# The border into the output projection of a hybrid decoder layer: other buffers, earlier loads, retention started later

## The chip, the cores and the metric

The kernel runs on one core of a Trainium2 chip. The metric is the device time of one execution in microseconds; the lower the better. Of the core's engines four matter here: TensorE (PE in the profile; its weight loads are PEld) multiplies matrices into the eight banks of PSUM, VectorE (DVE) does elementwise work, ScalarE (ACT) does copies, casts and functions, and the SyncE queue (SP) issues every DMA of this kernel. Each of these works through its own queue in order. GpSimd has no part in the stretch that is changed.

## The reference, cut to what matters

One decoder layer on 1024 tokens of width 1024, float32. A pre-norm feeds one input projection with six column groups of 1024:

```python
xn = rms_norm(h, norm_in_g)
proj = xn @ w_in                                  # 1024 x 6144
q, k, v, g_ret, x_lru, g_lru = split(proj)
o_ret = group_norm_heads(chunkwise_retention(rotary(q), rotary(k) * HD ** -0.5, v))   # 8 heads x 128
y_ret = o_ret * silu(g_ret)
o_lru = rg_lru(causal_depthwise_conv(x_lru, conv_w, conv_b), ...)    # gates, decay, scan
y_lru = o_lru * silu(g_lru)
h = h + concat([y_ret, y_lru]) @ w_out            # 2048 x 1024
return rms_norm(h, norm_out_g)
```

The retention goes over 8 chunks of 128 tokens; per chunk and head it needs the masked scores q·k, their product with v, the product of q with a state, and an update of that state from k and v.

## The kernel before, in words

**Stages.** First v is projected (`v_phase`), with the weights of w_in streamed. Then 20 "quads" follow, each 256 columns of the other five groups for all tokens, done as seven half-size products (P1 to P7, a Strassen-like scheme) of 12 matmuls each; twelve quads are for the LRU group and the two gates, the last eight for q and k. One `Runner.step` of a quad does p2, p6, p5, p7, then p1 of the *next* quad, then p4 and p3, and between these prepares the next quad's weights (`prep1` to `prep4`: sums, and splits into a high and a low part). Results go to DRAM scratch: v to `v_d`, rotated q and k to `qk_d`, the gate to `g_d`, the LRU output to `l_d`.

**The output projection** (lines 699 to 947) multiplies 8 token tiles by w_out in four passes: LRU rows with output columns 0 to 511, LRU rows with columns 512 to 1023 (`dh` 0 and 1), retention rows with the first half of the columns, and retention rows with the second. One unit (`unit_o`) is one token tile in one pass: 8 values of k by 3 matmuls (high by high, high by low, low by high), so 24 matmuls of 128x512. A weight slab (`slab`) is 256 rows of w_out, loaded into a `wraw` buffer and split into a high tile by ACT (line 106) and a low tile by DVE (line 107) in the pool `wo`; four slabs make a pass. A token tile (`y_tile`) is loaded into a `wraw` buffer too, from `l_d` or from `o_d`, and split in the same way into the pool `yl`. There are three `wraw` buffers. The residual input (`h`, line 885) is loaded behind the latest token tile and added when a unit is done.

**Retention** runs inside the passes. `pieces` makes 35 closures out of the two head halves a and b (`Retention(0)`, `Retention(1)`): the first, `first(a, 0)`, does loads, scores (line 787), transposes of k (794) and the copy `kn` (797); the second does `state` (808) and `out` (825, 826) of a's chunk 0; later ones alternate, and `first(r, n)` also flips chunk n-1 (847), multiplies it by the gate and stores it to `o_d`. `unit_o` calls `fill` after k = 3 and after k = 7; each call takes one closure off the list.

**SBUF.** The buffers of the quads and of the output projection share the right side of SBUF. For the quads, in order of address and in KB a partition: the operands of P1, P2, P6, P5, P7, P4, P3 (16 each, four tiles of 4), `slabs` (36), `raw` (two of 8, the incoming w_in), `sums` (8). This stack is closed, and over it lie, in the same order of address: `qkc` (16, incoming q and k of retention), `wraw` (12), `wo` (40), `yl` (64), `vc` (8), `h` (32); the total is 172 both times. A buffer can be written as soon as the old tile under it has been read for the last time. The last quad reads P1 first (a step early), then P2, P6, P5, P7, P4, P3. The small buffers of retention (`kn`, `sm`, `gch`, ...) lie on the left side over `w4`, which holds the last quads' q and k until they are rotated and stored.

**Order.** The framework plans the order of each engine's queue by its own estimate of times: among the instructions whose operands and buffers are free by that estimate, it takes the one written first. One that is written late but ready early is issued early. `tc.issue_after` ties an instruction behind another.

```python
    ...
        ("qkc", 4), ("wraw", 3), ("wo", 10), ("yl", 16), ("vc", 4), ("h", 8))}
    ...
    w_o = group(D, 0)
    ...
    load_yl(0)
    while fillers:
        fill()
    ...
    fillers.extend(pieces(Retention(0), Retention(1)))
```

Of the kernel before, what the change touches and what calls it, by code (L numbers as in the profile page):

```python
# [10 lines left out]
F32 = mybir.dt.float32  # L11
F32R = mybir.dt.float32r
I32 = mybir.dt.int32
AF = mybir.ActivationFunctionType
ALU = mybir.AluOpType

P = 128
T = 1024
D = 1024
NT = T // P  # L20
NK = D // P
# [19 lines left out]
def hybrid_layer(  # L41
# [17 lines left out]
    pe, act, dve, pool, sp = nc.tensor, nc.scalar, nc.vector, nc.gpsimd, nc.sync  # L59
# [7 lines left out]
    def pool_on(side, name, bufs):  # L67
        return tc.tile_pool(name=name, bufs=bufs, side=side, reuse_waits="tile")

    const = ctx.enter_context(tc.tile_pool(name="const", bufs=1, side="left"))  # L70
    small = ctx.enter_context(tc.tile_pool(name="small", bufs=4, side="left"))
# [3 lines left out]
    def psum():  # L75
        return ps_p.tile([P, 512], F32, name="pp", tag="pp")
# [28 lines left out]
    def split(src, hi, lo):  # L105
        act.copy(out=hi, in_=src)  # L106
        dve.tensor_tensor(out=lo, in0=src, in1=hi.bitcast(F32), op=ALU.subtract)  # L107
# [41 lines left out]
    rstd = const.tile([P, NT], F32, name="rstd")  # L149
# [8 lines left out]
    o_d = dram.tile([NT, P, 2, 4, P], F32, name="o_d")  # L158
    l_d = dram.tile([8, P, T], F32, name="l_d")
# [4 lines left out]
    raw = s_stack.enter_context(pool_on("right", "raw", 2))  # L164
# [317 lines left out]
    fillers = []  # L482

    def fill():
        if fillers:
            f = fillers.pop(0)
            if f:
                f()
# [205 lines left out]
    run = Runner(lq + qk_quads())  # L694
    while run.i < len(run.q):
        run.step()
    s_stack.close()

    op = {n: ctx.enter_context(pool_on("right", n, k)) for n, k in (
        ("qkc", 4), ("wraw", 3), ("wo", 10), ("yl", 16), ("vc", 4), ("h", 8))}  # L700
    def slab(row, col):
        r = op["wraw"].tile([P, 2, 512], F32, name="wor", tag="wor")
        sp.dma_start(out=r, in_=w_out[row:row + 256, col:col + 512]
                     .rearrange("(k p) c -> p k c", p=P))
        hi, lo = [op["wo"].tile([P, 2, 512], F32R, name="wo", tag="wo") for _ in range(2)]
        split(r, hi, lo)
        return [(hi[:, j], lo[:, j]) for j in range(2)]

    def group(row0, col, ks=range(0, NK, 2)):
        return [a for k in ks for a in slab(row0 + k * P, col)]  # L710

    last_load = [None]

    def y_tile(src):

        r = op["wraw"].tile([P, NK, P], F32, name="yraw", tag="wor")
        last_load[0] = sp.dma_start(out=r, in_=src)
        hi, lo = [op["yl"].tile([P, NK, P], F32R, name="yt", tag="yt") for _ in range(2)]
        split(r, hi, lo)
        return hi, lo  # L720

    hres = []
    for t in range(NT):
        r = op["h"].tile([P, T], F32, name="h", tag="h")
        hres.append(r)

    def unit_o(ps, y, wg, cols, fills=True):
        for k in range(NK):
            mm3(ps, tuple(a[:, k] for a in y), tuple(a[:, cols] for a in wg[k]), k == 0, k == NK - 1)
            if fills and k in (3, 7):  # L730
                fill()

    w_o = group(D, 0)
    yl = {}

    def load_yl(t):
        yl[t] = y_tile(l_d[:, :, t * P:(t + 1) * P].rearrange("k p c -> p k c"))

    def load_yr(t):
        yl[t] = y_tile(o_d[t].rearrange("p f h c -> p (f h) c"))  # L740

    load_yl(0)
    while fillers:
        fill()
    ph_stack.close()
# [106 lines left out]
    def pieces(a, b):  # L852

        def first(r, n):
            if n < NT:
                r.scores(n)
            if n:
                r.flip(n - 1)

        f = []  # L860
        for n in range(NT + 1):
            m = n - 1
            f.append(lambda n=n: first(a, n))
            if m >= 0:
                f.append(lambda m=m: first(b, m))
            if n < NT:
                f.append(lambda n=n: (a.state(n), a.out(n)))
            if m >= 0:
                f.append(lambda m=m: (b.state(m), b.out(m)))
        return f + [None, lambda: first(b, NT)]  # L870

    fillers.extend(pieces(Retention(0), Retention(1)))
    for dh in range(2):
        cols = slice(dh * HALF, (dh + 1) * HALF)
        w_cur = w_o
        nxt = (D, HALF) if dh == 0 else (0, 0)
        w_o = group(*nxt, (0,))
        for t in range(NT):
            if dh == 0 and t + 1 < NT:
                load_yl(t + 1)  # L880
            ps = psum()
            unit_o(ps, yl[t], w_cur, slice(0, HALF))
            r = hres[t][:, cols]
            with tc.issue_after(last_load[0].ins):
                sp.dma_start(out=r, in_=x[t * P:(t + 1) * P, cols])
            dve.tensor_tensor(out=r, in0=ps, in1=r, op=ALU.add)
            if dh == 1 and 0 < t < NT - 2:
                load_yr(t - 1)
            if t == NT - 2:
                w_o += group(*nxt, (2, 4, 6))  # L890
# [5 lines left out]
    def square(dst, src):  # L896
        junk = junkp.tile([P, 512], F32, name="junk", tag="junk")
        act.activation(out=junk[:, :src.shape[-1]], in_=src, func=AF.Square, accum_out=dst)  # L898

    w_cur, w_o = w_o, group(0, HALF, (0,))  # L900
    for t in range(NT):
        if t < 2:
            load_yr(t + 5)
        elif t == 3:
            while fillers:
                fill()
            load_yr(NT - 1)
        elif t == NT - 2:
            w_o += group(0, HALF, (2, 4, 6))
        ps = psum()  # L910
        unit_o(ps, yl[t], w_cur, slice(0, HALF))
        r = hres[t][:, :HALF]
        m = ssum[:, t, 0:1]
        dve.tensor_tensor(out=r, in0=ps, in1=r, op=ALU.add)  # L914
        square(m, r)
        dve.tensor_scalar(out=m, in0=m, scalar1=1.0 / D, scalar2=EPS, op0=ALU.mult, op1=ALU.add)
        dve.tensor_tensor(out=r, in0=r, in1=gain2[:, :HALF], op=ALU.mult)
    for t in range(NT):
        r = hres[t][:, HALF:]
# [14 lines left out]
        root = small.tile([P, 1], F32, name="root", tag="root")  # L934
# [82 lines left out]
```

## Time and profile before

| what | value |
|---|---|
| time, median of 3 runs | 767.24 us (765.67 to 769.76) |
| the profiled execution's own time | 765.5 us |
| its span (first to last instruction) | 763.7 us |
| PE matmul busy | 734.1 us, 96% of the span |
| DVE busy | 548.6 us, 72% |
| ACT busy | 413.4 us, 54% |
| mean granted TensorE clock | 0.993 |

The share of a chain or an engine is a mean over stages. To read a stage one takes a window of it: busy time of each engine, granted clock, and how much of the 16 DMA engines was in use. The page's strip of 40 slices (19 us each) shows PE at nine tenths or more except at both ends, in the two slices from 496 to 535 us (6 and 8) and in the one from 649 to 668 us (8).

### The profile page before, as it was taken

The numbers are of one execution on the slowest core, as the hardware profiler recorded it, in microseconds if no ns is written. First come the engines' busy times: TensorE is split into PE (matmuls) and PEld (weight loads), VectorE is DVE, ScalarE is ACT, GpSimd is POOL, SyncE is SP. The second block draws the span as 40 slices with busy tenths as digits, with TensorE's granted clock in tenths as the row PEclk, the third lists the DMA queues.
The fourth block names the chain that finished last, engine by engine and source line by source line (L and its number), as shares of the span: only waits on it lengthen the run. The fifth ranks groups of instructions, "written<-read, shape, count | busy, mean of one in ns | idle before, by whom it ended". The sixth has DMA issues, their size and how long they took to land.

```text
span 763.7 us, 9411 instructions
## 1 busy us (share of the span) xinstructions
PE 734.1 (96%) x3508; PEld 610.8 (80%) x3508; DVE 548.6 (72%) x918; ACT 413.4 (54%) x635; POOL 0.2 (0%) x4
## 2 busy tenths in 40 slices
PE   6999999999999999999999999968999999899996
PEld 5877888887787788788788888757888898788885
DVE  6998647669977968977899888585567665652443
ACT  7784436695599679679533333255435443431332
POOL 0000000000000000000000000000000000000000
PEclk9999999999999999999999999999999999999999
DMA  9752712141214212421445542789946556331022
GB/s 317 268 191 88 245 53 70 56 128 38 72 52 161 74 55 87 148 83 52 169 122 126 134 110 56 226 266 323 313 146 206 194 179 235 97 129 36 28 88 106
DMA packets 85406, 105.58 MB, mean 138 GB/s; under 512 B 4848, under 2 KB 58224, under 8 KB 85360
## 3 DMA queue, kind: packets, MB, share of 16 engines
q1 hardware_dynamic: 85360, 104.99, 43.0%
q8 instruction: 27, 0.44, 0.2%
q14 instruction: 19, 0.16, 0.1%
HBM read 75.61 MB, written 29.36 MB: 137 GB/s over the span
## 4 chain that ended last, share of the span: by engine, by line
PE 67%; DVE 13%; ACT 10%; DMA 5%; issue 4%; SPq 0%; DVEq 0%; ACTq 0%
PE pp L112 59%; PE pp L826 2%; DVE xc L561 2%; PE pp L825 2%; PE pp L808 2%; PE pp L787 2%; DMA yraw<-l_d 2%; DVE wq L107 1%; ACT wq L106 1%; PE pp L847 1%; DVE y L614 1%; DVE wl L107 1%; DMA rot<-in_rot_t 1%; ACT L643 1%; PE pp L794 1%
## 5 line engine op out<-in xcount | busy, mean ns | idle before, releaser
L112 PE MATMUL pp<-wh,wq 128*128 128x512 f32 x960 | 301.6, 391 | 1.6 <-ACT cy L470 0.7
L112 PEld LDWEIGHTS pp<-wh,wq 128*128 128x128 f32 x960 | 179.9, 188 | 42.9 <-ACT cy L461 2.2
L112 PE MATMUL pp<-wo,yt 128*128 128x512 f32 (+1 forms) x792 | 186.1, 390 | 3.9 <-ACT yt L106 3.9
L112 PE MATMUL pp<-wl,wq 128*128 128x512 f32 x480 | 186.9, 389 | 0.0
L112 PEld LDWEIGHTS pp<-wo,yt 128*128 128x128 f32 x792 | 143.4, 189 | 31.6 <-ACT yt L106 4.3
L112 PEld LDWEIGHTS pp<-wl,wq 128*128 128x128 f32 x480 | 90.1, 188 | 18.5
L107 DVE TENSOR_TENSOR wq<-t,wq 128x1024 fp32r<-128x1024 f32 x40 | 48.7, 1221 | 39.1 <-ACT wq L106 32.1
L106 ACT CAST wq<-t 128x1024 fp32r<-128x1024 f32 x40 | 41.7, 1049 | 31.3 <-PE pp L112 26.7
L112 PE MATMUL pp<-wh 128*128 128x512 f32 x112 | 45.6, 407 | 8.0 <-ACT wh L106 8.0
L112 PE MATMUL pp<-wh,w 128*128 128x512 f32 x160 | 52.9, 391 | 0.1
L112 PE MATMUL pp<-wl,wh 128*128 128x512 f32 x112 | 44.8, 401 | 0.0
L112 PE MATMUL pp<-wh,wl 128*128 128x512 f32 x112 | 44.1, 398 | 0.0
L898 ACT ACTIVATE junk<-h 128x512 f32<-128x512 f32 (+1 forms) x17 | 10.3, 607 | 49.8 <-DVE h L914 25.3
L461 ACT COPY cy<-pp 128x512 f32<-128x512 f32 x20 | 11.6, 581 | 46.1 <-PE pp L112 45.5
L112 PEld LDWEIGHTS pp<-wh,w 128*128 128x128 f32 x160 | 30.0, 188 | 6.9 <-DVE w L107 0.6
L112 PEld LDWEIGHTS pp<-wh 128*128 128x128 f32 x112 | 21.8, 195 | 13.2 <-ACT wh L106 8.4
L112 PE MATMUL pp<-wl,w 128*128 128x512 f32 x80 | 31.1, 389 | 0.0
L839 ACT ACTIVATE yn<-pp,nb,rs_y 128x128 f32<-128x128 f32 x64 | 24.1, 458 | 11.8 <-DVE nb L837 11.8
L470 ACT COPY cy<-pp 128x512 f32<-128x512 f32 x20 | 11.6, 578 | 29.4 <-PE pp L112 29.3
L422 ACT CAST wq<-wraw 128x512 fp32r<-128x512 f32 x40 | 22.9, 617 | 8.3 <-PE pp L112 7.4
L97 ACT ACTIVATE rs_s<-ve 128x4 f32<-128x4 f32 x16 | 3.2, 202 | 43.8 <-DVE ve L832 43.8
L424 DVE TENSOR_TENSOR wq<-wraw,wq 128x512 fp32r<-128x512 f32 x40 | 26.7, 681 | 0.1
(154 smaller groups left out, 1116.2 us busy)
## 6 DMA issues: line engine op xcount, KB each, us to landing
wraw<-in_w_in SPq DMA_DIRECT2D x40, 512.0 KB, 4.7
qkc<-qk_d SPq DMA_DIRECT2D x16, 512.0 KB, 5.1
wor<-in_w_out SPq DMA_DIRECT2D x16, 512.0 KB, 5.7
bt<-in_w_in SPq DMA_DIRECT2D x20, 256.0 KB, 5.4
xA<-in_xT SPq DMA_DIRECT2D x16, 256.0 KB, 5.4
v_d<-vo SPq DMA_DIRECT2D x16, 256.0 KB, 2.4
xt<-in_x SPq DMA_DIRECT2D x8, 512.0 KB, 3.3
l_d<-y SPq DMA_DIRECT2D x8, 512.0 KB, 3.2
```

Source lines behind the costliest of these rows:

```text
L106: act.copy(out=hi, in_=src)
L107: dve.tensor_tensor(out=lo, in0=src, in1=hi.bitcast(F32), op=ALU.subtract)
L112: pe.matmul(ps, a, b, start=first and j == 0, stop=last and j == 2, skip_group_check=True)
L422: act.copy(out=h[:, j], in_=b)
L424: dve.tensor_tensor(out=l[:, j], in0=b, in1=h[:, j].bitcast(F32), op=ALU.subtract)
L461: act.copy(out=self.cy[:, :TH], in_=self.A)
L561: dve.scalar_tensor_tensor(out=xc[:, d:], in0=c[:, :T - d], scalar=cw[3 - d], in1=xc[:, d:], op0=ALU.mult, op1=ALU.add)
L787: heads(lambda h, hs: pe.matmul(psc[:, hs], k[:, hs], q[:, hs], start=True, stop=True))
L808: heads(lambda h, hs: pe.matmul(pkv[:, hs], kn[:, hs], vn[:, hs], start=True, stop=True))
L825: pe.matmul(po[:, hs], q[:, hs], st[:, h], start=True, stop=False)
L826: pe.matmul(po[:, hs], sm[:, h], vn[:, hs], start=st is None, stop=True)
L839: heads(lambda h, hs: act.activation(out=yn[:, hs], in_=po[:, hs], func=AF.Identity, scale=rs[:, h:h + 1], bias=nb[:, h:h + 1]))
```

## The change

The order of the pools on the right side becomes `wraw`, a new pool `y0` of two tiles, `wo`, `qkc`, `yl` (now 14), `vc`, `h`. So the staging buffers and the first token tile lie over the operands that the last quad reads first, and `qkc` moves from P1's place to the end of P5's and to P7's. Half of the first weights is loaded into a `raw` tile before the quads' stack is closed. The first token tile is loaded ahead of the weights, the second ahead of the loop. A square root of one column is written there as well. The first slab for the second pass is loaded in unit 2, not ahead of unit 0. Retention's list gets three empty entries, so its first closure comes in unit 1 and its second in unit 2, and the third and fourth closures change places. In the third pass the loads of token tiles 5 to 7 stand at units 0, 2, 4 (before: 0, 1, 3), and the rest of the list is emptied at unit 4.

```diff
+    early = raw.tile([P, 2, 2, 512], F32, name="early", tag="raw")
+    for j in range(2):
+        row = D + (4 + 2 * j) * P
+        sp.dma_start(out=early[:, j], in_=w_out[row:row + 256, 0:512].rearrange("(k p) c -> p k c", p=P))
     s_stack.close()
 
     op = {n: ctx.enter_context(pool_on("right", n, k)) for n, k in (
-        ("qkc", 4), ("wraw", 3), ("wo", 10), ("yl", 16), ("vc", 4), ("h", 8))}
-    def slab(row, col):
-        r = op["wraw"].tile([P, 2, 512], F32, name="wor", tag="wor")
-        sp.dma_start(out=r, in_=w_out[row:row + 256, col:col + 512]
-                     .rearrange("(k p) c -> p k c", p=P))
+        ("wraw", 3), ("y0", 2), ("wo", 10), ("qkc", 4), ("yl", 14), ("vc", 4), ("h", 8))}
+    def slab(row, col, r=None):
+        if r is None:
+            r = op["wraw"].tile([P, 2, 512], F32, name="wor", tag="wor")
+            sp.dma_start(out=r, in_=w_out[row:row + 256, col:col + 512]
+                         .rearrange("(k p) c -> p k c", p=P))
...
-    def y_tile(src):
-
+    def y_tile(src, t):
+
+        pl = "yl" if t else "y0"
...
-        hi, lo = [op["yl"].tile([P, NK, P], F32R, name="yt", tag="yt") for _ in range(2)]
+        hi, lo = [op[pl].tile([P, NK, P], F32R, name="yt", tag=pl) for _ in range(2)]
...
-    w_o = group(D, 0)
...
     load_yl(0)
+    w_o = group(D, 0, (0, 2))
+    for j in range(2):
+        w_o += slab(None, None, early[:, j])
+    load_yl(1)
+    act.activation(out=small.tile([P, 1], F32, name="root", tag="root"), in_=rstd[:, 0:1],
+                   func=AF.Sqrt)
     while fillers:
         fill()
...
-    fillers.extend(pieces(Retention(0), Retention(1)))
+    p_a, p_b, *rest = pieces(Retention(0), Retention(1))
+    rest[0], rest[1] = rest[1], rest[0]
+    fillers.extend([None, None, p_a, None, p_b] + rest)
     for dh in range(2):
...
-        w_o = group(*nxt, (0,))
+        if dh == 1:
+            w_o = group(*nxt, (0,))
         for t in range(NT):
-            if dh == 0 and t + 1 < NT:
+            if dh == 0 and 0 < t < NT - 1:
                 load_yl(t + 1)
+            if dh == 0 and t == 2:
+                w_o = group(*nxt, (0,))
...
-        if t < 2:
-            load_yr(t + 5)
-        elif t == 3:
+        if t == 4:
             while fillers:
                 fill()
-            load_yr(NT - 1)
+        if t in (0, 2, 4):
+            load_yr(t // 2 + 5)
         elif t == NT - 2:
```

## Rows read from the trace of the kernel before

**Rows 1.** Busy time of each engine in stretches around the border (the view by windows): stretch, its length, busy time and instructions of PE, PEld, DVE, ACT, POOL, then the granted clock, the share of the DMA engines in use and GB/s.

```profile
456.00:470.00 14.00, 14.00 (x64) 11.58 (x63) 11.88 (x15) 5.54 (x9) 0.00 (x0) 1.00 0.19 48
470.00:485.00 15.00, 15.00 (x68) 12.43 (x67) 8.47 (x10) 3.68 (x6) 0.00 (x0) 1.00 0.64 176
...
500.00:515.00 15.00, 9.02 (x38) 7.16 (x36) 13.09 (x13) 7.96 (x11) 0.00 (x0) 0.89 0.96 294
515.00:530.00 15.00, 11.68 (x71) 9.84 (x72) 7.50 (x21) 8.31 (x19) 0.00 (x0) 1.00 1.04 311
```

**Rows 2.** The same view, cut at the end of the last quad's last matmul, at the point from which PE is full again, and near the end.

```profile
500.30:533.30 33.00, 23.71 (x126) 19.88 (x127) 22.98 (x35) 18.09 (x32) 0.00 (x0) 0.95 1.01 310
...
533.30:657.30 124.00, 124.00 (x801) 111.72 (x800) 75.32 (x279) 52.42 (x132) 0.00 (x0) 1.00 0.62 204
...
671.80:757.00 85.20, 85.15 (x401) 71.26 (x399) 35.63 (x89) 25.15 (x56) 0.00 (x0) 1.00 0.22 78
```

**Rows 3.** Who waited for whom from 485 to 534 us: total us, times, longest.

```profile
ACT yt L106 <- DMA yraw<-l_d: 6.3, 4, 4.6
...
PE pp L112 <- ACT yt L106: 3.9, 1, 3.9
...
PE pp L847 <- ACT yn L839: 2.9, 1, 2.9
...
PE pp L808 <- ACT kn L797: 2.2, 1, 2.2
...
PE pp L112 <- ACT cy L470: 0.7, 1, 0.7
```

**Rows 4.** The group of the projection's matmuls among PE's groups from 500.3 to 533.3 us.

```profile
L112 PE MATMUL pp<-wo,yt 128*128 128x512 f32 x60 | 16.7, 422 | 3.9 <-ACT yt L106 3.9
```

**Rows 5.** Two pieces of the chain of waits where PE runs without a gap: start, length, what.

```profile
528.31 0.89 PE pp L787 x8
...
529.64 2.77 PE pp L112 x12
```

**Rows 6.** The SP queue in order of time: start, us, line, what it loads or stores.

```profile
476.23 1.99 SPq L772 DMA_DIRECT2D qkc<-qk_d  x3
485.52 1.41 SPq L703 DMA_DIRECT2D wor<-in_w_out  x3
...
496.73 0.37 SPq L703 DMA_DIRECT2D wor<-in_w_out  x1
497.87 0.37 SPq L717 DMA_DIRECT2D yraw<-l_d  x1
...
512.56 1.48 SPq L682 DMA_DIRECT2D qk_d<-cy  x1
...
518.29 0.84 SPq L772 DMA_DIRECT2D qkc<-qk_d  x2
```

**Rows 7.** DMA issues of the whole run: number, KB each, median us from issue to landing.

```profile
qkc<-qk_d SPq DMA_DIRECT2D x16, 512.0 KB, 5.1
wor<-in_w_out SPq DMA_DIRECT2D x16, 512.0 KB, 5.7
...
yraw<-l_d SPq DMA_DIRECT2D x8, 512.0 KB, 6.3
```

**Rows 8.** DVE in order of time: the reads of the `raw` tiles of the last two quads (lines 415 and 424), and the end of the last quad.

```profile
453.76 0.68 DVE L424 TENSOR_TENSOR wq<-wraw,wq 128x512 fp32r<-128x512 f32 x1
...
458.48 0.68 DVE L415 TENSOR_TENSOR t<-wraw 128x512 f32<-128x512 f32 x1
...
472.80 0.68 DVE L424 TENSOR_TENSOR wq<-wraw,wq 128x512 fp32r<-128x512 f32 x1
...
500.33 0.69 DVE L480 TENSOR_TENSOR cy<-pp,cy 128x512 f32<-128x512 f32 x1 [1.35 <-PE pp L112]
...
509.87 1.22 DVE L679 TENSOR_TENSOR cx<-cx,t 128x1024 f32<-128x1024 f32 x1
```

**Rows 9.** ACT in order of time; in brackets the idle time ahead and what ended it.

```profile
493.91 0.59 ACT L470 COPY cy<-pp 128x512 f32<-128x512 f32 x1 [4.85 <-PE pp L112]
...
521.95 1.28 ACT L97 ACT_TABLE_LOAD   x1
524.01 0.20 ACT L97 ACTIVATE rs_s<-ve 128x4 f32<-128x4 f32 x1 [0.78 <-DVE ve L832]
```

**Rows 10.** All engines in order of time where the second pass goes over into the third (an SP issue, an ACT cast, a PE transpose).

```profile
661.05 0.38 SPq L703 DMA_DIRECT2D wor<-in_w_out  x1
...
665.14 1.04 ACT L106 CAST wo<-wor 128x1024 fp32r<-128x1024 f32 x1 [2.17 <-DMA wor<-in_w_out]
...
666.60 0.33 PE L847 MATMUL pp<-ident,yn 128*128 128x128 f32 x1 [2.22 <-ACT yn L839]
```

**Rows 11.** Instructions in order of time from the start: a function of line 231, which is written behind the whole v stage; the two `diag` tiles of line 215, which are `raw` tiles; and the first load of a quad's weights into a `raw` tile.

```profile
2.49 0.21 ACT L231 ACTIVATE sp_a<-par_sb 128x8 f32<-128x8 f32 x1 [0.48 <-DMA par_sb<-in_par]
...
72.84 1.30 DVE L215 TENSOR_TENSOR diag<-ident,rstd 128x512 f32<-128x512 f32 x2
...
74.81 0.94 SPq L394 DMA_DIRECT2D wraw<-in_w_in  x2
```

**Rows 12.** The last retention tile: its store on SP, and the cast of the token tile that is loaded from it.

```profile
679.48 0.32 SPq L850 DMA_DIRECT2D o_d<-ot  x1
...
684.82 1.05 ACT L106 CAST yt<-yraw 128x1024 fp32r<-128x1024 f32 x1 [2.85 <-DMA yraw<-o_d]
```

More of the change, by code (lines that the diff above doesn't have):

```diff
@@ L731, in unit_o @@
                 fill()
-    w_o = group(D, 0)
     yl = {}
     def load_yl(t):
-        yl[t] = y_tile(l_d[:, :, t * P:(t + 1) * P].rearrange("k p c -> p k c"))
+        yl[t] = y_tile(l_d[:, :, t * P:(t + 1) * P].rearrange("k p c -> p k c"), t)
     def load_yr(t):
-        yl[t] = y_tile(o_d[t].rearrange("p f h c -> p (f h) c"))
+        yl[t] = y_tile(o_d[t].rearrange("p f h c -> p (f h) c"), t)
     load_yl(0)
+    w_o = group(D, 0, (0, 2))
[4 more added lines that the diff above has]
+                   func=AF.Sqrt)
     while fillers:
```

## The prediction

> **What bounds the kernel now.** I read the busy time by stretch first. PE is busy without a gap before 493 us, again from 533 to 657 us, and from 672 us to the last unit [rows 1, 2]. There the time is the number of matmuls, and nothing that another engine does matters until it makes PE wait. So the change can only give what PE loses in between, and can only cost where it makes new holes. The big hole is 500.3 to 533.3 us: 33.0 us with 23.7 us busy, 9.3 us idle [rows 2]. The waits say at whom: 3.9 us at the first matmul of the projection, for the cast of the first token tile; 2.2 us for retention's `kn`; 2.9 us for `yn`; and a little ahead of it 0.7 us for a copy of the last quad [rows 3]. ACT is behind all of them, and ACT itself waited 6.3 us for token tiles to land. The SP queue says why they land late: staging lies over P2's operands, so the first three slabs are issued at 485.5 us, the next one at 496.7 and the first token tile at 497.9 [rows 6], while the DMA engines were in use at 0.19 and 0.64 before and at 0.96 to 1.04 afterwards [rows 1].
>
> **How much the hole holds.** 126 matmuls lie in it [rows 2], 60 of them 128x512 [rows 4]. Without gaps 12 of those take 2.77 us (0.231 each) and 8 small ones 0.89 us (0.111 each) [rows 5]: 60 x 0.231 + 66 x 0.111 = 13.9 + 7.3 = 21.2 us. The hole is worth 33.0 - 21.2 = 11.8 us: 9.3 us idle, and 2.5 us in which matmuls run stretched, part of it at a granted clock of 0.89, a mean between the engine's two levels [rows 1].
>
> **The change, part by part.**
>
> *Staging over P1.* The free date of P1's place is seen in the three `qkc` loads that lie there now: 476.2 us, against 485.5 for P2's [rows 6]. So the first token tile and two slabs start 9.3 us earlier, land by about 476.2 + 2 + 6.3 = 484.5 [rows 6, 7], and are split while DVE and ACT have room. The other two slabs sit in a `raw` tile whose last read by the quad before ends at 454.4 us (453.76 + 0.68 [rows 8]); their 1 MB goes out in a stretch with the DMA engines at 0.19 [rows 1]. Price of these moves: nothing, as every load now runs under quads on which PE is full; if that cover were gone it would be one load, 5.7 us [rows 7]. The splits need their `wo` tiles, over P2, P6 and P5; P7, the product after P5, is done when its copy starts at 493.9 us [rows 9], so those are free by then. The second token tile lies over P7 and P4, free between 493.9 and 500.3. So at 500.3 us PE finds its operands, runs units 0 and 1 at once, and the 3.9 us go. Six casts of about 1.04 us [rows 10] move ahead of 500 us on ACT. One of them can stand in front of the copy at 493.9, behind which PE waits 0.7 us already [rows 3]: -0.7 (projection matmuls fill that gap) to +1.0 us; I take 0, as the row has the copy start as soon as its product ends.
>
> *Retention later.* Unit 0 takes 24 x 0.231 = 5.5 us, so `first(a, 0)` comes at 500.3 + 5.5 + 2.8 = 508.6 us. `state` and `out` of a's chunk 0 come a unit later, after 1.3 us of scores and transposes and 5.5 us of projection, at 515.4, `first(b, 0)` at 515.4 + 1.8 + 2.8 = 520.0. This gives `kn` and `yn` cover, which had none. The moved `qkc` loads start at 491 to 494 us and take 5.1 us [rows 7]: well before 508.6, cost nothing. What is late next is b's first q and k. They are read back from DRAM after the last quad's rotation. Now DVE ends that at 511.1 us [rows 8], the last store is issued at 512.6, and the load at 518.3 [rows 6], landing at 523.4. The subtraction and six operations of up to 1.22 us are 8.0 us without splits in between, so with these gone from DVE the rotation would end near 508 us and, with SP no longer behind late loads, b's load start 3 to 4 us sooner; it lands between 519.4 and 523.4 for a need at 520.0: 0 to 3.4 us, I take 1.5.
>
> *`kn` and `yn` behind other people's loads.* ACT takes its queue in order, and loads that are not urgent (token tiles 4 to 7, residual tiles) still go out as early as they can. A cast that waits for one of them holds `kn` or `yn` behind it. Bounds: 0, or the 2.2 + 2.9 = 5.1 us of today [rows 3]; I take 1.5, as three token tiles fewer are under way after 500 us.
>
> *The pass changes.* Before the third pass PE waits 2.2 us for `yn`, which stands on ACT behind the cast of a slab that was issued at 661.05 and not needed before the last pass [rows 10]. With the list three closures later another closure stands there, an `out` that needs no `yn`. I take the 2.2 us as gone, and 0.5 us (bounds 0 to 2.2) as coming back at one of the two changes of pass that carry retention.
>
> *The shift at the end.* Three closures more lie in the third pass. PE is full there (85.15 of 85.20 us [rows 2]), and their matmuls are only moved. The last token tile is cast 684.8 - 679.5 = 5.3 us after its store is issued [rows 12] and needs a split of some 2.3 us more; between the last flip, now in unit 2, and unit 7 lie four units, 22 us. Cost nothing.
>
> *The square root.* The first table load for it takes 1.28 us on ACT, and ACT then still idles 0.78 us for DVE before the function can run [rows 9]: it is hidden now. The added instruction depends on `rstd` alone. The planner issues such work as soon as it is ready: line 231, written behind the whole v stage, ran at 2.5 us [rows 11]. So I expect the added root near 73 us, and the table load to stay where it is. By rows it is worth 0 to 1.28 us, and I take 0. The Trainium skill (ScalarE: Activation LUTs, What ACT_TABLE_LOAD costs) gives a switch of tables as some 1.28 us of load and 1.38 us of drain; the trace agrees with the load and shows no drain of that size between 523.2 and 524.0 us. By the page alone a preload that stayed in place would give another 2.7 us.
>
> **Sum.** 11.8 + 2.2 - 1.5 - 1.5 - 0.5 = 10.5 us. The profiled execution took 765.5 us, 1.8 us around its span of 763.7, so 755.0 on its scale. The median of the runs is 1.7 us above it: 767.2 - 10.5 = 756.7 us. Best case: 11.8 + 2.2 + 0.7 = 14.7, so 752.5. For the likeliest case I let half of the remaining bounds come true: about 752.5 to 761.
>
> **The rivals.**
>
> *A, the forecast:* the hole closes but for 3 to 4 us. For it: each date above lies ahead of its need, and the DMA engines have idle time to move into. 0.62.
>
> *B, the hole moves into retention's start:* the projection starts at 500.3, but b's load and ACT's order come out at their upper ends: 14.0 - 3.4 - 5.1 = 5.5 us gained, 761.7. For it: today's two retention waits are of just this kind, and DMA stays busy. Against: two more units of cover. 0.17.
>
> *C, no change:* as B, with the copy at 493.9 held by a cast (1.0) and 2.2 us at each of two pass changes: 14.0 - 8.5 - 1.0 - 4.4 = 0.1 us, 767.1. Against: four independent places at their worst at once. That the DMA engines at 1.01 over the hole [rows 2] bound it as such speaks for C too; yet about 2.5 MB (two slabs, three token tiles) leave it, 8 us at 310 GB/s, so that alone would land at B. 0.12.
>
> *D, slower:* the early load takes one of the two `raw` buffers long before the last quad. It has no input but w_out, so the planner could send it whenever a buffer is free, and hold it until the splits at 490 us. The quads would run on one buffer: a quad reads its own from 458.5 to 473.5, 15.0 us, then 0.9 us of issue and 5.1 to 5.7 us of landing (other loads of 512 KB) follow, 21.0 to 21.6 us in a cycle of 472.80 - 453.76 = 19.04 us [rows 7, 8, 11]. That is some 2 us for each of 19 quads, 38 us; even at half of it, 767.2 - 10.5 + 19 = 775.7. It decides if the early load is issued before about 454 us. Against it: at 72.8 us both `raw` tiles were kept for the `diag` tiles written earlier, and the quad's load, which needed nothing else, was issued only at 74.8 [rows 11]; buffers seem to be given out in the order written. 0.09, with any other way of getting slower.
>
> That the change doesn't do what it says can hold for the square root alone; it is in A and changes no time there.
>
> **Range and chances.** 0.5% (about what a measurement of this kernel can tell from no change) is 3.8 us, so faster means under 763.4 and slower over 771.1. All of A and nearly all of B are faster: 0.79. C: 0.13. D: 0.08. The range from 752 to 765 holds A and B and leaves out D, most of C and a little below A.
>
> **What would show it.** Early load issued between 454 and 472 us; first token tile at 476 to 478 and its cast before 490; first projection matmul by 500.6 us; in the 33 us after the last quad PE busy at least 29 us, its clock at 1.00; the first closure's scores near 508.6; no 2.2 us in front of the flip at the pass change. Wrong would be: PE waiting for `kn`, `yn` or b's scores for over 6 us together, a token tile landing after 500 us for units 0 to 2, or gaps in the quads.

## The result, and the profile after

The changed kernel took 756.18 us (median, 755.79 to 757.44); the kernel before, run beside it, 768.5 us (765.67 to 770.43). The ratio is 0.9845, with an interval from 0.9809 to 0.9882: 1.55% faster, on the side that the forecast of 756.7 us stood on. A second measurement (below) gave 758.42 us beside 768.17 us, 1.26% faster. The profiled spans are 763.7 us before and 754.4 us after.

The first lines of the page of the kernel after: span, then busy time of each engine.

```profile
span 754.4 us, 9420 instructions
...
PE 731.9 (97%) x3508; PEld 609.9 (81%) x3508; DVE 547.8 (73%) x918; ACT 414.5 (55%) x637; POOL 0.2 (0%) x4
```

The same number of matmuls, in 9.3 us less. The gain of the stretch itself is larger. DVE of the kernel after in order of time: the last quad's last subtraction, and the last operation of its rotation.

```profile
502.52 0.69 DVE L480 TENSOR_TENSOR cy<-pp,cy 128x512 f32<-128x512 f32 x1 [3.18 <-PE pp L112]
...
510.07 1.22 DVE L679 TENSOR_TENSOR cx<-cx,t 128x1024 f32<-128x1024 f32 x1
```

In this execution the last quad ended 2.2 us later than in the profiled execution before (502.5 us, not 500.3 us), and from the start of that subtraction to the end of the span it is 754.4 - 502.5 = 251.9 us, against 763.7 - 500.3 = 263.4 us before [rows 8]: 11.5 us. I use this "border to end" below, since it leaves out how early the quads end, which differs by over 3 us between executions (500.1 to 503.8 us, leaving out one run that slowed the quads on purpose). It flatters the change a little: in the kernel after, six matmuls of the projection (1.4 us) run ahead of the border. They put the quad's end off by 0.7 us and take 1.4 us from what is left behind it.

The view by windows of the kernel after (stretch, length, busy time and instructions of PE, PEld, DVE, ACT, POOL, granted clock, DMA share, GB/s), to be held against [rows 1, 2].

```profile
502.30:535.30 33.00, 30.31 (x174) 26.41 (x173) 22.50 (x41) 16.12 (x30) 0.00 (x0) 1.00 0.98 310
...
456.00:470.00 14.00, 14.00 (x64) 11.58 (x63) 10.31 (x14) 5.32 (x8) 0.00 (x0) 1.00 0.56 148
```

In the 33 us behind the last quad PE is now busy 30.31 us with 174 matmuls; it was 23.71 us with 126. The granted clock is 1.00, where it was 0.95. The transfers that moved are seen in the share of the DMA engines from 456 to 470 us: 0.56, where it was 0.19. Behind the quad that share is about as high as before, 0.98, where it was 1.01.

Who waited for whom in the kernel after from 487 to 536 us: total, times, longest.

```profile
PE pp L799 <- DMA qkc<-qk_d: 2.7, 1, 2.7
```

This is PE's only wait there. The 3.9 us for the token tile, the 2.2 us for `kn`, the 2.9 us for `yn` and the 0.7 us for the copy [rows 3] are gone. Left is the read-back of b's first q and k.

The SP queue of the kernel after in order of time, against [rows 6].

```profile
458.24 2.15 SPq L701 DMA_DIRECT2D early<-in_w_out  x2
...
479.17 0.37 SPq L724 DMA_DIRECT2D yraw<-l_d  x1
...
512.64 1.32 SPq L682 DMA_DIRECT2D qk_d<-cy  x1
514.00 2.54 SPq L787 DMA_DIRECT2D vc<-v_d  x2
...
518.09 0.36 SPq L784 DMA_DIRECT2D qkc<-qk_d  x1
```

The early load goes out at 458.24 us, the first token tile at 479.17. b's first q and k are loaded at 518.09; between the last store of the rotation (512.64) and that load SP issues loads of v, of the residual input and of the gate without a pause.

PE of the kernel after in order of time: start, length, line, operation; in brackets the idle time ahead and what ended it.

```profile
495.52 1.52 PE L112 MATMUL pp<-wo,yt 128*128 128x512 f32 x6
...
502.32 6.96 PE L112 MATMUL pp<-wo,yt 128*128 128x512 f32 x30
509.13 1.05 PE L799 MATMUL pp<-qkc 128*128 128x128 f32 x8
...
523.30 1.16 PE L799 MATMUL pp<-qkc 128*128 128x128 f32 x8 [2.69 <-DMA qkc<-qk_d]
...
527.49 1.05 PE L799 MATMUL pp<-qkc 128*128 128x128 f32 x8
...
665.11 1.38 PE L859 MATMUL pp<-ident,yn 128*128 128x128 f32 x4 [0.99 <-ACT yn L851]
```

Six projection matmuls run before the last quad's end: they fill the gap of 0.7 us where PE had waited for the copy and push the quad's last matmuls back by the other 0.7 us. The projection goes on without a break at 502.32, the first scores come at 509.13. The second wait is the one for `yn` at the change into the third pass: 0.99 us, where it was 2.22 [rows 10].

### The profile page after: what moved, and what is told of

Same layout as the page of the kernel before. It is cut to its first block, busy times and chain, and to the rows that moved or that the text cites. A ratio compares the mean times of both kernels' runs of the same rounds, so it can differ in the third digit from the quotient of the medians.

```text
span 754.4 us, 9420 instructions
## 1 busy us (share of the span) xinstructions
PE 731.9 (97%) x3508; PEld 609.9 (81%) x3508; DVE 547.8 (73%) x918; ACT 414.5 (55%) x637; POOL 0.2 (0%) x4
## 4 chain that ended last, share of the span: by engine, by line
PE 65%; DVE 14%; ACT 10%; DMA 5%; issue 3%; SPq 1%; ACTq 0%; DVEq 0%
PE pp L112 58%; DVE xc L561 2%; PE pp L838 2%; PE pp L799 1%; PE pp L820 1%; PE pp L837 1%; DVE wq L107 1%; DVE y L614 1%; ACT wq L106 1%; DMA vc<-v_d 1%; DMA rot<-in_rot_t 1%; PE pp L859 1%; DVE wl L107 1%; ACT L643 1%; DMA graw<-in_gate_w 1%
## 5 line engine op out<-in xcount | busy, mean ns | idle before, releaser
L112 PE MATMUL pp<-wo,yt 128*128 128x512 f32 (+1 forms) x792 | 183.8, 387 | 0.0
L461 ACT COPY cy<-pp 128x512 f32<-128x512 f32 x20 | 11.6, 580 | 41.8 <-PE pp L112 41.2
L107 DVE TENSOR_TENSOR yt<-yraw,yt 128x1024 fp32r<-128x1024 f32 x16 | 19.5, 1222 | 9.1 <-ACT yt L106 9.1
L112 PEld LDWEIGHTS pp<-wl,wh 128*128 128x128 f32 x112 | 21.7, 194 | 5.2 <-DVE wl L107 0.4
```

The source lines that it names most:

```text
L112: pe.matmul(ps, a, b, start=first and j == 0, stop=last and j == 2, skip_group_check=True)
L461: act.copy(out=self.cy[:, :TH], in_=self.A)
```

## The experiments

The prediction had credited the staging with the 3.9 us and the spacing of the list with cover for `kn` and `yn`, as parts of one sum. The theory to be tested was that the parts add up so; the rivals were B and C, in which one part alone brings little or the transfers bind. Ten more kernels were run, always beside the kernel before, and the kernel after and the one with one more slot a second time. None leaves computation out, except that one omits a square root whose result nothing uses. Each ratio is to the kernel before as it ran beside that kernel (medians 767.6 to 768.7 us). "Border to end" is taken from each one's profiled execution, which is not always a typical one: that of "one more slot" took 757.33 us, the slowest of its five. Six matmuls lie ahead of the border in all of them but the kernel before, "old pools" and "spacing alone" (none) and "no early weights" (four).

| kernel | median us (range) | ratio to before, interval | border to end, us |
|---|---|---|---|
| before | 768.5 (765.67 to 770.43) | 1 | 263.4 |
| after | 756.18 (755.79 to 757.44) | 0.9845 [0.9809, 0.9882] | 251.9 |
| after, measured again | 758.42 (756.2 to 761.04) | 0.9874 [0.9852, 0.9895] | 254.4 |
| no spacing | 767.27 (764.73 to 771.14) | 0.9977 [0.9956, 0.9997] | 263.6 |
| old pools | 757.75 (755.61 to 760.22) | 0.9857 [0.9832, 0.9881] | 256.1 |
| no early weights | 762.31 (761.39 to 763.61) | 0.9915 [0.9896, 0.9934] | 260.2 |
| spacing alone | 760.58 (759.99 to 762.67) | 0.99 [0.9879, 0.9922] | 258.0 |
| one more slot | 752.4 (752.22 to 757.33) | 0.9817 [0.9794, 0.984] | 251.8 |
| no exchange | 758.17 (756.84 to 760.14) | 0.9879 [0.9862, 0.9896] | 254.5 |
| buffer held | 762.11 (760.37 to 763.8) | 0.9928 [0.9908, 0.9949] | 256.6 |
| cx products early | 757.34 (756.25 to 758.04) | 0.9864 [0.9849, 0.9879] | 254.5 |
| one more slot, again | 753.31 (751.63 to 754.99) | 0.9809 [0.9792, 0.9826] | 249.1 |
| no square root | 757.33 (755.55 to 759.38) | 0.9862 [0.9841, 0.9882] | 255.3 |
| slot and cx early | 752.84 (751.63 to 754.05) | 0.9802 [0.9788, 0.9817] | 249.4 |

**No spacing.** Everything of the change but the list:

```diff
-    p_a, p_b, *rest = pieces(Retention(0), Retention(1))
-    rest[0], rest[1] = rest[1], rest[0]
-    fillers.extend([None, None, p_a, None, p_b] + rest)
+    fillers.extend(pieces(Retention(0), Retention(1)))
```

> The changed kernel with retention's list as it was: no empty entries, no exchange of the third and fourth closure. Theory (operands in time, and retention's latency covered by two more units): the projection still starts without a wait at the quads' end, but kn, yn and b's first scores stand in PE's queue before they can be ready. b's first q and k land near 523 us as in the changed kernel, and are wanted near 516 to 518; PE waits 5 to 8 us in all between 500 and 535 us, against 2.7 in the changed kernel; time 758.5 to 762. Rival (the border is bound by the bytes moved, so the earlier loads are the whole gain): PE waits as in the changed kernel, 755.5 to 757.5.

Measured: 767.27 us. Both expectations missed; some 1.5 us of the gain are left by the medians (768.74 us beside it; 0.2 to 3.4 us by the interval). PE in order of time in this kernel:

```profile
501.43 1.52 PE L112 MATMUL pp<-wo,yt 128*128 128x512 f32 x6
502.79 1.05 PE L799 MATMUL pp<-qkc 128*128 128x128 f32 x8
...
512.75 2.07 PE L820 MATMUL pp<-vc,kn 128*128 128x128 f32 x8 [5.69 <-ACT kn L809]
...
527.34 0.33 PE L859 MATMUL pp<-ident,yn 128*128 128x128 f32 x1 [3.77 <-ACT yn L851]
```

And its ACT queue over the same stretch:

```profile
509.09 1.05 ACT L106 CAST yt<-yraw 128x1024 fp32r<-128x1024 f32 x1 [3.11 <-DMA yraw<-l_d]
511.02 1.41 ACT L788 ACTIVATE vc<-vc,rstd 128x512 f32<-128x512 f32 x2 [0.89 <-DMA vc<-v_d]
512.34 1.12 ACT L809 ACTIVATE kn<-pp,cst_sb 128x128 f32<-128x128 f32 x4
...
520.89 1.05 ACT L106 CAST yt<-yraw 128x1024 fp32r<-128x1024 f32 x1 [7.43 <-DMA yraw<-l_d]
```

The two v tiles that ACT scales there (line 788) are issued on SP here:

```profile
503.34 1.57 SPq L787 DMA_DIRECT2D vc<-v_d  x2
```

The projection does start at once, so the staging does its work: the wait for the first token tile is gone. But scores stand 1.2 us behind the quad (501.6), and the first state needs `kn`. PE wants it 5.5 us behind the quad, where it was 12.6 us before, and it is ready 11.1 us behind, where it was 14.8. On ACT `kn` stands behind a cast that waits 3.11 us for a token tile of a later unit, and then behind the scaling of v, for which ACT waits another 0.89 us: the load of v, issued at 503.34, lands at 511.0. That is the wait that ends last, so without that cast ahead of it on ACT `kn` would have come no sooner. The second such cast holds ACT for 7.43 us with the copy of the state behind it, and DVE for 9.2 us at the low part of the same tile, with the statistics behind it that the root and `yn` need. What the staging gives back, retention takes: this is ACT's order, one half of the rival B's mechanism (PE does not wait for b's load here), and in size the rival C's.

**Old pools.** The two pools in the old order, the rest of the change kept:

```diff
-        ("wraw", 3), ("y0", 2), ("wo", 10), ("qkc", 4), ("yl", 14), ("vc", 4), ("h", 8))}
+        ("qkc", 4), ("wraw", 3), ("y0", 2), ("wo", 10), ("yl", 14), ("vc", 4), ("h", 8))}
```

> The changed kernel with staging back over P2 and qkc back over P1; the early tile, the order of the loads and the spacing stay. Theory: the first token tile is issued 9 us later, near 488 us, and still lands by 494; half of the first weights is in the early tile and the other half lands by 495, so all is split near the quads' end: first wait of PE 0 to 1.5 us, time 756 to 758.5. Rival (where staging lies is the heart of the change): the loads crowd at the border again as before, 3 to 5 us of waits at the first projection matmuls, time 760 to 764.

Measured: 757.75 us, as the theory had it; it does not separate from the two measurements of the kernel after, 756.18 and 758.42. The one difference of over 0.5 us that its waits show is the 0.7 us in front of the last quad's last products, which is back. So with the early weights, the new order of the loads and the spacing present, the place over P1 is worth some 1.6 us or nothing, not the 3.9 us.

**No early weights.** All four slabs of the first weights through the three staging buffers:

```diff
-    w_o = group(D, 0, (0, 2))
-    for j in range(2):
-        w_o += slab(None, None, early[:, j])
+    w_o = group(D, 0)
```

> The changed kernel without the early tile: all four first slabs go through the three staging buffers, over P1, behind the first token tile. Theory: the last two slabs and the second token tile are issued when a staging buffer is split, near 494 to 498 us, and are ready near 503 to 508 for a need at 505 (third slab) and 508 us (second token tile): PE waits 0 to 4 us more than in the changed kernel, time 756.5 to 760. Rival (bytes bound the border): 1 MB more inside it at some 310 GB/s is 3.4 us more, time 759 to 760.5.

Measured: 762.31 us, some 5 us slower than the kernel after and slower than both expected. PE in order of time:

```profile
502.52 1.66 PE L112 MATMUL pp<-wo,yt 128*128 128x512 f32 x6 [0.45 <-DVE wo L107]
504.45 4.14 PE L112 MATMUL pp<-wo,yt 128*128 128x512 f32 x17 [0.26 <-ACT yt L106]
...
525.27 2.08 PE L793 MATMUL pp<-qkc 128*128 128x128 f32 x8 [4.86 <-DMA qkc<-qk_d]
```

The small waits at the projection's start are under 1 us together. The rest is the wait for b's q and k, 4.86 us and then matmuls at half speed (8 scores in 2.08 us, not 1.16 us). Two slabs fewer to fetch after 490 us are worth most there, at the load that is last; how much of it is this execution's own is open, as that wait was 2.7 and 4.1 us in two executions of the kernel after.

**Spacing alone.** The kernel before, with the list and the three loads of the third pass as in the change:

```diff
-    fillers.extend(pieces(Retention(0), Retention(1)))
+    p_a, p_b, *rest = pieces(Retention(0), Retention(1))
+    rest[0], rest[1] = rest[1], rest[0]
+    fillers.extend([None, None, p_a, None, p_b] + rest)
```

> The kernel before with the list of retention as changed (three empty entries, the exchange) and the token loads of the third pass moved with it; pools, staging and order of loads as before. Theory: the 3.9 us at the first projection matmul stay, since the loads are late as before, but kn and yn get cover: of 5.1 us of waits there 3 to 5 go, as does most of the 2.2 us at the change of pass; time 3 to 7 us under the kernel before, 760 to 765. Rival (bytes bound the border): 0 to 2 us under the kernel before.

Measured: 760.58 us (768.74 us beside it), as expected: about 8 us. Two of its waits from 440 us on:

```profile
PE pp L112 <- ACT yt L106: 4.5, 2, 3.9
...
PE pp L847 <- ACT yn L839: 0.5, 1, 0.5
```

The 3.9 us are there, the wait for `kn` is gone and that for `yn` nearly. So the list alone gives about 8 us and the rest alone 1 to 2 us. Both together gave 12.3 us in the first measurement and 9.8 us in the second, so whether the parts add up to less than the whole is not settled by the medians. What the waits show is narrower: the rest alone takes away waits of 3.9 + 0.7 us and brings 1 to 2 us, since PE only meets the next wait sooner; on top of the list it brings 2 to 4 us.

**One more slot.** The only wait left behind the quad was b's load. An empty entry in front of `first(b, 0)`:

```diff
-    fillers.extend([None, None, p_a, None, p_b] + rest)
+    fillers.extend([None, None, p_a, None, p_b, None] + rest)
```

(The text on record calls the closure ahead of it the first of the second half; it is the state and output of a's chunk 0.)

> The kernel after, with one more empty slot behind the first piece of the second half, so that everything from the second half's first loads on stands a slot later. Theory (retention's first pieces run behind their producers, and a slot of projection between pieces is what covers that): the scores' wait of 2.7 us for qkc at about 523 us goes, the flip's wait of 1.0 us stays or goes, and the time falls by 1.5 to 3.5 us against the kernel after, to 753 to 755 us. Rival (the chain's end is set by the number of slots left, and the last pieces spill behind the projection): the 2.7 us go, but pieces left over at the end of the pass run bunched together and cost 2 us or more, so 756 to 759 us.

Measured: 752.4 us, and in a second measurement beside the kernel after:

> The kernel with one more empty slot once more, beside the kernel after on one chip. Theory (the slot takes 2 to 4 us of waits away): 752 to 754 us, 2 to 4 us under the kernel after. Rival (the first measurement's five runs, 752.2 to 757.3 us, were of a better hour): within 1.5 us of the kernel after.

> The kernel after, unchanged, as the measure for the three runs beside it: 755.5 to 757.5 us.

753.31 us against 758.42 us: 5.1 us, more than the wait of 2.7 us. The 33 us behind the last quad in the second measurement's profile (columns as above):

```profile
501.40:534.40 33.00, 32.90 (x186) 28.34 (x185) 22.78 (x41) 15.86 (x30) 0.00 (x0) 1.00 0.95 294
```

And b's first scores on PE there, which carry no wait:

```profile
523.08 1.16 PE L799 MATMUL pp<-qkc 128*128 128x128 f32 x8
```

PE is busy 32.90 us of 33.00 us, with 186 matmuls in place of 174. Why the slot is worth more than the wait is seen in the kernel after, measured again. PE in order of time there:

```profile
522.63 1.69 PE L799 MATMUL pp<-qkc 128*128 128x128 f32 x8 [4.08 <-DMA qkc<-qk_d]
...
528.46 1.05 PE L799 MATMUL pp<-qkc 128*128 128x128 f32 x8
```

And windows of the same execution, the 33 us behind its last quad and three of 3 us:

```profile
500.43:533.43 33.00, 28.91 (x151) 24.93 (x151) 19.84 (x34) 15.68 (x30) 0.00 (x0) 0.95 0.93 291
...
522.00:525.00 3.00, 2.37 (x13) 2.37 (x14) 0.64 (x2) 0.00 (x0) 0.00 (x0) 0.68 1.11 354
525.00:528.00 3.00, 3.00 (x12) 2.40 (x11) 0.12 (x2) 2.79 (x9) 0.00 (x0) 0.75 1.06 363
528.00:531.00 3.00, 3.00 (x23) 2.79 (x22) 2.28 (x3) 1.64 (x5) 0.00 (x0) 1.00 0.87 267
```

In the 33 us PE is busy 28.91 us, where the first profile has 30.31. The wait is 4.08 us, and from b's scores to the next scores it takes 528.46 - 522.63 = 5.83 us, against 527.49 - 523.30 = 4.19 us in the first profile of the same kernel: the granted clock is 0.68 and 0.75 over 6 us, a mean between the engine's two levels. The wait costs 2.7 us in one execution and 4.1 + 1.6 = 5.7 us in another. The extra slot takes both away in its second profile; in its first, of the slowest execution, 0.8 us of the wait were left, with the clock at 1.00. This version beats the kernel before and the kernel after.

**No exchange.** The line that changes the third and fourth closures left out:

```diff
-    rest[0], rest[1] = rest[1], rest[0]
```

(The closures exchanged are `first(a, 1)` and `first(b, 0)`; the text on record misnames the second.)

> The kernel after, without the exchange of the third and fourth pieces: the scores of the first half's second tile are issued ahead of the state and output of its first. Theory (the empty slots are what matters): within 1 us of the kernel after, 755.5 to 757.5 us. Rival (the exchange is what gives kn and yn their cover): a wait of 2 us or more for kn or yn returns beside the first state or the first flips, and the time is 758 to 761 us.

Measured: 758.17 us, just inside the rival's range, which doesn't separate from the two measurements of the kernel after, 756.18 and 758.42. The wait that the rival named is there, but in place of the other. From its waits behind the border:

```profile
PE pp L859 <- ACT yn L851: 4.8, 2, 4.0
```

No wait for `qkc` is left in this kernel: b's scores come a closure later and find their data, and a's flip comes a closure sooner and finds no `yn`. The exchange trades one wait for the other.

**Buffer held.** The loads of the early weights written ahead of the first quad, so that they hold one of the two `raw` buffers through all quads:

```diff
+    early = raw.tile([P, 2, 2, 512], F32, name="early", tag="raw")
+    for j in range(2):
+        ...
     lq = lru_quads()
...
-    early = raw.tile([P, 2, 2, 512], F32, name="early", tag="raw")
-    ...
```

> The kernel after, with the early token tile's place taken from the quads' raw buffers before the first quad instead of after the last one, so that the quads' weight loads have a buffer less for the whole stretch of the quads. The prediction's rival D priced this place at 38 us whole and 19 us at half. Theory (a place is a place: each quad's load waits for the one before to be read): 775 to 795 us, with waits of TensorE for wq and of VectorE for wraw in the quads. Rival (the loads are far enough ahead that one buffer fewer is covered): 756 to 759 us.

Measured: 762.11 us. Neither expectation holds, and the price of the rival D, 38 us or 19 us, is far off. The load was issued at 73.7 us, so the quads did run on one buffer. A late stretch of quads by windows:

```profile
400.00:460.00 60.00, 60.00 (x266) 49.67 (x266) 52.67 (x62) 18.12 (x27) 0.00 (x0) 1.00 0.42 108
```

A quad's load on SP:

```profile
461.87 2.62 SPq L394 DMA_DIRECT2D wraw<-in_w_in  x2
```

The last read of the quad before on DVE, and the first and last of this one:

```profile
460.15 0.69 DVE L434 TENSOR_TENSOR t<-wraw 128x512 f32<-128x512 f32 x1
...
468.33 0.69 DVE L415 TENSOR_TENSOR t<-wraw 128x512 f32<-128x512 f32 x1 [1.28 <-DMA wraw<-in_w_in]
...
479.96 0.69 DVE L434 TENSOR_TENSOR t<-wraw 128x512 f32<-128x512 f32 x1
```

PE is busy 60.00 of 60.00 us. (In the first quads it did lose some: from 80 to 100 us it was busy 18.20 us.) The cycle is the load's issue, 6.5 us later the first read, 12.3 us later the last one's end: 18.8 us, and 19.8 us from last read to last read, in which the work of a quad fits. The prediction had taken the 15.0 us of reading [rows 8] for fixed; that was how long the reads were spread when nothing pressed, and they drew together, to 12.3 us here. The 4 to 6 us that the kernel did lose are seen as a late end of the quads (505.4 us) and as a wait of 4.3 us for b's load behind them, with the clock at 0.81 and 0.84 in the two stretches of 10 us from 520 us; why the load came later there was not tried.

**cx products early.** b's load waits for the rotation's writes, and these for DVE. In the last quad the two products that need only cx were moved ahead of the quad's last matmuls, into DVE's idle time; the order of the last writes, cx and cy, changes with it:

```diff
             q.p4()
+            if n is None:
+                q.post_x = post_x(q)
...
+    def post_x(q):
+        tx = big(name="t")
+        dve.tensor_tensor(out=tx, in0=q.cx, in1=rot[1], op=ALU.mult)
+        dve.tensor_tensor(out=q.cx, in0=q.cx, in1=rot[0], op=ALU.mult)
+        return tx
```

> The kernel after, with the last quad's two products of cx moved in front of the quad's last matrix products, into VectorE's idle 3.18 us before 502.5 us. The same arithmetic, two instructions earlier. Theory (the second half's first load waits for the rotation's writes, and these for VectorE's six instructions behind the quad): the rotation ends some 2.3 us sooner, about 509 us in place of 511.3, the 2.7 us wait for qkc falls to 0 to 1 us, and the time falls by 1.5 to 2.7 us, to 753.5 to 754.7 us. Rival (that load is held by transfers ahead of it in the queue, by landing times rather than by the rotation): the wait stays above 2 us and the time stays at 755.5 to 756.5 us.

Measured: 757.34 us, the rival's side. DVE's last rotation instruction:

```profile
506.51 1.22 DVE L682 TENSOR_TENSOR cy<-cy,t 128x1024 f32<-128x1024 f32 x1
```

b's load on SP:

```profile
514.80 0.32 SPq L799 DMA_DIRECT2D qkc<-qk_d  x1
```

b's first scores on PE:

```profile
521.51 2.08 PE L814 MATMUL pp<-qkc 128*128 128x128 f32 x8 [2.47 <-DMA qkc<-qk_d]
```

The quad ended 1.3 us sooner in this execution, so the rotation's end at 507.7 us is 2.3 us sooner behind its last subtraction than in the kernel after, as meant. The load was issued 2 us sooner behind the quad, and then took 6.7 us to land where it had taken 5.2 us (6.6 us in the second profile of the kernel after): the wait hardly moved. With the extra slot as well there is nothing left to shorten:

> One more empty slot and the last quad's two cx products early, together. Theory (the slot alone has taken the waits, so an earlier rotation gives nothing more): 751.5 to 754 us, as with the slot alone. Rival (the two add): 750 to 751.5 us. Third (the earlier writes crowd the transfers, as the single run with the products early showed): 754.5 to 757 us.

Measured: 752.84 us, as with the slot alone.

**No square root.** The instruction left out; its result goes nowhere.

> The kernel after without the early square root; its result is used by nothing, so the outputs are computed in full. Theory (it floats to about 73 us and fetches no table for retention): the table load stays beside the last quad's end or retention's start, and the time is within 1 us of the kernel after. Rival (it saves a table load at retention's start): 1.3 us or more slower.

Measured: 757.33 us, within the two measurements of the kernel after. In the kernel after it ran near the start, with a table load of its own, and the load beside retention stayed. ACT of the kernel after in order of time:

```profile
68.13 1.28 ACT L753 ACT_TABLE_LOAD   x1
...
73.03 0.20 ACT L753 ACTIVATE root<-rstd 128x1 f32<-128x1 f32 x1 [3.62 <-DVE rstd L206]
...
521.20 1.28 ACT L97 ACT_TABLE_LOAD   x1
522.50 0.20 ACT L97 ACTIVATE rs_s<-ve 128x4 f32<-128x4 f32 x1
```

## Why the prediction was right, and which steps of it were not

**The sum.** 10.5 us were forecast. The profiled stretch from the border to the end became 11.5 us shorter; the medians differ by 12.3 us, and by 9.8 us in the second measurement. By the steps: 11.8 us of the hole, less 2.7 for b's load, plus 2.2 - 1.0 at the change of pass, plus 0.7 for the filled gap, are 11.0 us; from border to end the six matmuls of that gap count 1.4 and not 0.7, so 11.7 us stand against the 11.5. That 756.7 us came so near to 756.18 is in part luck: 1.5 us booked for `kn` and `yn` did not come and the gap gave 0.7, while b's load took 1.2 more than booked and the change of pass 0.5 more.

**The hole** held as sized: in the first profile all of its 11.8 us but the 2.7 came back, and with one more slot those too. What was to be seen of it was seen there: PE busy 30.31 us (at least 29 was said), the clock at 1.00. The second profile of the same kernel just misses both, 28.91 us at 0.95. The first scores came at 509.1 us, and 508.6 was said, but for a quad that ends at 500.3: behind the quad's end it was 6.6 us, not 8.3, because six matmuls of the projection had run before it.

**Staging over P1**, which "so at 500.3 us PE finds its operands" rested on, was right in its dates (token tile issued at 479.2 us, projection without a break) and wrong in its weight. Without the spacing it is worth 1 to 2 us in all, and in the full change its place is worth some 1.6 us or nothing. The step that failed is the one that booked its price and gain by itself: the 3.9 us were not independent of what follows them.

**"This gives `kn` and `yn` cover, which had none"** is one sentence in the prediction; the list that it speaks of gave two thirds of the gain or more alone. The bound that stood beside it, "0, or the 2.2 + 2.9 = 5.1 us of today", would not have held without that cover: there the two waits are 5.69 and 3.77 us. With the spacing they were 0 behind the quad, where 1.5 us were booked.

**b's load** was named as the next thing to be late, rightly, and its term was mis-sized: 1.5 us booked, bounds 0 to 3.4; measured 2.7, 3.6 and 4.1 us in three executions of the same code but for the square root, with up to 2.6 us more for the clock behind it. The landing lay within what was said, 20.8 to 22.2 us behind the quad's end (519.4 to 523.4 us is 19.1 to 23.1 behind 500.3), though the rotation ended 8.8 us behind it and not 7.7 (one token tile's split still stood among its operations) and SP issued the load, after other loads of 4 us, 15.6 us behind it and not 14 to 15; whether another order on SP would help was not tried. What failed is the need: PE came to b's scores 18.1 us behind the quad in all three, not 19.7, since the six matmuls had run ahead. So what the gap at the copy gave is in part lost again here. And an earlier rotation alone does not cure it: with the early products the load was issued 2 us sooner behind the quad and landed at most 0.5 us sooner.

**The gap at the copy** was taken as 0 and gave 0.7, its best bound: six projection matmuls fill it. **The change of pass** left 0.99 us where 0.5 was booked (0.5 us in the second profile). **The square root** floated to the start and changed nothing, as said. The Trainium skill (ScalarE: Activation LUTs, What ACT_TABLE_LOAD costs) gives 1.28 us of load and 1.38 us of drain; the load agrees again, and the function now starts 0.02 us behind it (522.50 against 521.20 + 1.28), with no drain in between.

**The rivals.** What one half of the change alone does (no spacing) is B's wait for ACT's order, so that part of its mechanism was real, and the other half is what keeps it away. C's other ground, that the DMA engines at a share of 1.01 bound the hole as such, fell: the share is 0.98 now, and 48 more matmuls run in the same 33 us. D did not occur: the early load was issued at 458.24 us, behind the last reads of the quad before; and its price was wrong.

## What to carry to other kernels

Work brought forward on the critical engine pays in full only if its next operands are ready too: here 4.6 us of removed waits brought 1 to 2 us by themselves. Before crediting a removed wait, follow the engine to the next thing it would then reach early, and price the two edits together. A filler slot between a producer and its consumer was the cheapest cover here (about 8 us for the list, about 5 us for one slot more), and one more should be tried as long as a wait for a just-written operand is left. A buffer's reading time in a trace is not its least: 15.0 us of it became 12.3 us under pressure.

## What the runs showed of the hardware that was not expected

A stall of PE can cost more than its length, but does not always. After 3.62 us of waiting in the kernel without the square root PE ran at the lower of its two levels; windows of that kernel:

```profile
522.00:525.00 3.00, 1.02 (x5) 1.02 (x6) 0.88 (x6) 0.44 (x2) 0.00 (x0) 0.60 1.02 389
525.00:528.00 3.00, 3.00 (x13) 2.71 (x13) 0.76 (x2) 1.06 (x4) 0.00 (x0) 0.50 1.09 358
...
531.00:534.00 3.00, 3.00 (x22) 2.75 (x22) 2.06 (x3) 1.69 (x6) 0.00 (x0) 1.00 0.33 122
```

PE in order of time there:

```profile
523.98 2.07 PE L797 MATMUL pp<-qkc 128*128 128x128 f32 x8 [3.62 <-DMA qkc<-qk_d]
...
526.56 4.32 PE L112 MATMUL pp<-wo,yt 128*128 128x512 f32 x12
530.72 1.05 PE L797 MATMUL pp<-qkc 128*128 128x128 f32 x8
```

From scores to scores it is 530.72 - 523.98 = 6.74 us, 2.6 us more than the 4.19 us of the kernel after, whose stall of 2.69 us left the clock at 1.00. A stall of 2.47 us (the cx products early) was followed by eight scores in 2.08 us, the lower level, so the length of the wait alone does not decide it. The Trainium skill (TensorE: Matmul & The Clock Gate, The HAM clock gate) has the lower clock as the default, from which activity releases the engine; the trace agrees so far, as the clock comes back to 1.00 once PE has run without a gap again (531 to 534 us above). What decides between the two outcomes of a stall of this length was not tried.

The other surprise is how far one load's landing varies in the same kernel: from issue to the scores that it releases it was 523.30 - 518.09 = 5.2 us in one profile of the kernel after, and 522.63 - 516.00 = 6.6 us in the other, with the DMA engines full both times (share 0.95 and 0.96 in the stretch). The two medians of that kernel lie 2.2 us apart, and a forecast of this border can't be finer than that.
